# A planner that puts projection products between the steps of four mixers: what is owed is paid in runs instead of piece by piece

## The chip, the cores and the metric

The kernel runs on one core of a Trainium2 chip. The metric is the device time of one execution in microseconds (us), the median of several runs. TensorE multiplies matrices, VectorE (DVE in the profile), ScalarE (ACT) and GpSimd (POOL) do the elementwise work, and DMA queues bring the weights.

## The reference, cut to what matters

One sequence of 512 tokens with 1024 features goes through two layers and then a second block; each has a token mixer and a feed-forward network. All is float32. What the change touches is the mixers, each of which is an input projection followed by work on the projected columns:

```python
z = x @ w_in                        # layer 0: 27 column tiles of 128
y_a = _rwkv7_time_mix(z[..., :RWKV_PROJ_COLS], ...)   # 8 heads of 64, a recurrence over tokens
y_b = moba(...)                     # 4 heads of 128, softmax attention
h = concatenate([y_a, y_b]) @ w_out
...
z = x @ w_in                        # layer 1: 40 column tiles, dilated attention, 8 heads
...
proj = a @ w_in                     # second block: 25 column tiles
y = concatenate([s5(...), hgrn2(...), fox(...), mlstm(...)]) @ w_out
```

## The kernel before

A float32 product is made from three passes: the weights and the activations are each split into a high part in the format fp32r and a remainder, and high times high, high times low and low times high are summed. A **piece** of a projection is the product of one 128x128 block of weights with all 512 tokens, so three matmuls of 512 columns (lines 273 to 275 in `stream`). Eight pieces make one column tile, a task; the weights of the next task are fetched at the first piece and split on ScalarE (line 229) and VectorE (line 231) at the seventh. After a piece `stream` yields 0.64, which is its length in the planner's units. `early` yields pieces of the output projection in the same way (lines 357 to 359).

The mixers are Python generators, called chains. Each step of a chain issues some instructions and yields a pair: what it costs TensorE, and how long until the chain's next step can start, both in the planner's units. The products of a chain are small and plain float32: 16 matmuls of 64x64 (line 560), 64 of 32x32 (lines 611 and 625), four transposes of 128x128 (line 448) and so on.

`race` writes out the order. It keeps a clock `t`, a time `ready` for each chain and a debt `owed`. A chain's step on TensorE adds `keep` times its cost to `owed`; a piece takes 0.64 off it, never below zero. Before each chain step the planner chooses: it issues a piece when no chain is live, when the earliest chain is not ready at `t`, or when `owed` is over 0.6. There are three races: one for layer 0 with five chains (four parts of RWKV, called core, tail with its gate, prep and inner, and the attention heads; keep is 0.65), one for layer 1 with a single chain of heads (keep 0.5), and one for the second block with two chains (keep 0.5). When a stream of pieces is exhausted, `over` supplies the pieces of `early`.

The order that `race` writes is a priority. The framework's own scheduler, while the program is built, places each engine's instructions by that priority as its estimate of readiness allows; on the chip each engine takes its instructions in the order placed, apart from weight loads on TensorE that overlap the products before them.

Of the kernel before, what the change touches and what calls it, by code (L numbers as in the profile page):

```python
# [106 lines left out]
class Kern:  # L107
# [198 lines left out]
    def race(self, chains, over, keep, hop, ls):  # L306


        t, owed, ready, waits, waited, stuck = 0.0, 0.0, [0.0] * len(chains), set(), set(), 0
        while any(chains):  # L310
            ready += [t] * (len(chains) - len(ready))
            live = [i for i, c in enumerate(chains) if c and i not in waits]
            i = min(live, key=lambda j: ready[j]) if live else None
            if self.gemm is not None and (i is None or ready[i] > t or owed > 0.6):
                r = next(self.gemm, None)
                if r is None:
                    self.gemm = over()
                    waits.clear()
                    continue
                if r:  # L320
                    t, owed, stuck = t + r, owed - r, 0
                    owed = max(owed, 0)
                    waits.clear()
                    continue
            if i is None:
                stuck += 1
                assert stuck < 3
                waits.clear()
                continue
            r = next(chains[i][0], 0)  # L330
            if r == 0:
                chains[i].pop(0)
                waits.clear()
            elif r is None:
                waits.add(i)
                waited.add(i)
            else:
                if i in waited:
                    waited.discard(i)
                    ready[i] = max(ready[i], t)  # L340
                at = max(t, ready[i]) if r[0] else ready[i]
                if r[0]:
                    t = at + r[0]
                    owed += keep * r[0]
                ready[i] = at + max(r[0], ls * r[1]) + hop
        while self.gemm is not None:
            if next(self.gemm, None) is None:
                self.gemm = over()
# [2028 lines left out]
```

## Time and profile before

| | |
|---|---|
| median of 3 runs | 2213.09 us (2209.51 to 2214.09) |
| profiled execution | 2210.03 us, its span 2207.9 us |
| busy, of the span | TensorE 97%, VectorE 57%, ScalarE 34%, GpSimd 16% |
| first race | from about 7 us to 397 us; pieces of `stream` until 327 us |
| second race | about 793 to 1119 us |
| third race | about 1498 to 1785 us |

In the rows below a duration of a matmul is partly modelled, and matmuls overlap: what one costs is read from its start to the start of the next one. "x16" in a row of a timeline is 16 instructions in one row, from the first start to the last end.

### The profile page before, as it was taken

What the parts mean: (1) busy time and instruction counts of PE and PEld (TensorE: products, weight loads), DVE (VectorE), ACT (ScalarE), POOL (GpSimd) and SP (SyncE); (2) the same over time, 40 slices, a digit from 0 to 9 for tenths busy, and PEclk for the clock granted to TensorE, in tenths of its full rate; (3) what the DMA queues carried; (4) which work ended last, traced back from release to release, by engine and by line L of the source; (5) the groups of instructions that cost most, each with busy time, mean ns of one, the idle gap of its engine ahead of it and who ended that gap; (6) DMA issues with size and microseconds to landing.
All of it is one profiled execution on the core that took longest, in us unless ns stands there. A gap on an engine that the chain in (4) does not pass through costs nothing.

```text
span 2207.9 us, 37394 instructions
## 1 busy us (share of the span) xinstructions
PE 2146.2 (97%) x15646; PEld 1701.9 (77%) x15646; DVE 1259.3 (57%) x2536; ACT 756.1 (34%) x1214; POOL 363.3 (16%) x391
## 2 busy tenths in 40 slices
PE   8999999999999999999999999998999999999998
PEld 6666667888878787777788888877677778888886
DVE  6575666764444666656474444466856576344445
ACT  4332333423332433333342233235434353222221
POOL 0011011370046433233220000011320021000000
PEclk9999999999999999999999999998999999999999
DMA  4111114333333422222243233213211232232321
GB/s 143 46 44 41 40 44 177 97 121 98 101 101 110 128 81 77 68 77 67 87 139 96 91 98 94 93 44 134 64 49 49 86 112 90 95 97 96 99 81 38
DMA packets 56088, 192.80 MB, mean 87 GB/s; under 512 B 8208, under 2 KB 8720, under 8 KB 55408
## 3 DMA queue, kind: packets, MB, share of 16 engines
q1 hardware_dynamic: 52384, 184.11, 25.9%
q0 software_dynamic: 3536, 6.32, 0.9%
q8 instruction: 122, 2.00, 0.4%
q14 instruction: 46, 0.38, 0.1%
HBM read 181.98 MB, written 8.39 MB: 86 GB/s over the span
## 4 chain that ended last, share of the span: by engine, by line
PE 79%; DVE 11%; issue 4%; ACT 3%; DMA 2%; POOL 1%; SPq 0%; DVEq 0%; ACTq 0%; POOLq 0%
PE gemm L273 6%; PE mlpo L357 6%; PE mlpo L358 6%; PE mlpo L359 6%; PE gemm L274 5%; PE gemm L275 5%; PE mlps L250 5%; PE mlps L251 5%; PE mlps L252 5%; PE ffg L251 2%; PE ffg L252 2%; PE ffg L250 2%; PE ffu L251 2%; PE ffu L252 2%; PE ffu L250 2%
## 5 line engine op out<-in xcount | busy, mean ns | idle before, releaser
L229 ACT CAST wh<-wr 128x1024 fp32r<-128x1024 f32 (+1 forms) x311 | 323.2, 1043 | 758.2 <-PE mlpo L359 241.4
L231 DVE TENSOR_TENSOR wl<-wr,wh 128x1024 fp32r<-128x1024 f32 (+1 forms) x285 | 353.1, 1240 | 354.3 <-ACT wh L229 268.2
L273 PE MATMUL gemm<-acth,wh 128*128 128x512 f32 (+1 forms) x672 | 302.6, 450 | 8.8 <-ACT acth L239 7.5
L275 PE MATMUL gemm<-acth,wl 128*128 128x512 f32 (+1 forms) x672 | 268.9, 400 | 4.4 <-DVE wl L231 4.4
L357 PE MATMUL mlpo<-wh,mlph 128*128 128x512 f32 x688 | 270.1, 393 | 0.2 <-DVE xres L1035 0.2
L274 PE MATMUL gemm<-actl,wh 128*128 128x512 f32 (+1 forms) x672 | 269.7, 401 | 0.0
L358 PE MATMUL mlpo<-wl,mlph 128*128 128x512 f32 x688 | 269.5, 392 | 0.0
L359 PE MATMUL mlpo<-wh,mlpl 128*128 128x512 f32 x688 | 269.4, 392 | 0.0
L250 PE MATMUL mlps<-acth,wh 128*128 128x512 f32 x448 | 176.3, 394 | 0.0
L252 PE MATMUL mlps<-acth,wl 128*128 128x512 f32 x448 | 176.2, 393 | 0.0
L251 PE MATMUL mlps<-actl,wh 128*128 128x512 f32 x448 | 176.1, 393 | 0.0
L273 PEld LDWEIGHTS gemm<-acth,wh 128*128 128x128 f32 (+1 forms) x672 | 126.9, 189 | 56.2 <-issue 19.5
L231 POOL TENSOR_TENSOR wl<-wr,wh 128x1024 fp32r<-128x1024 f32 (+1 forms) x26 | 68.5, 2653 | 553.7 <-ACT wh L229 508.2
L275 PEld LDWEIGHTS gemm<-acth,wl 128*128 128x128 f32 (+1 forms) x672 | 127.1, 189 | 34.9 <-DVE wl L231 5.4
L357 PEld LDWEIGHTS mlpo<-wh,mlph 128*128 128x128 f32 x688 | 129.4, 188 | 29.3 <-ACT mlph L239 0.4
L359 PEld LDWEIGHTS mlpo<-wh,mlpl 128*128 128x128 f32 x688 | 129.1, 188 | 29.1 <-DVE mlpl L240 0.2
L358 PEld LDWEIGHTS mlpo<-wl,mlph 128*128 128x128 f32 x688 | 129.2, 188 | 28.5
L274 PEld LDWEIGHTS gemm<-actl,wh 128*128 128x128 f32 (+1 forms) x672 | 127.7, 190 | 22.4 <-issue 4.6
L1035 DVE SCALAR_TENSOR_TENSOR xres<-xres,mlpo 128x512 f32<-128x512 f32 x120 | 82.1, 685 | 105.2 <-PE mlpo L359 104.1
L252 PEld LDWEIGHTS mlps<-acth,wl 128*128 128x128 f32 x448 | 84.1, 188 | 19.7
L251 PEld LDWEIGHTS mlps<-actl,wh 128*128 128x128 f32 x448 | 84.2, 188 | 19.5
L250 PEld LDWEIGHTS mlps<-acth,wh 128*128 128x128 f32 x448 | 84.1, 188 | 19.5
(613 smaller groups left out, 3874.9 us busy)
## 6 DMA issues: line engine op xcount, KB each, us to landing
wr<-mlp_w SPq DMA_DIRECT2D x128, 512.0 KB, 3.6
wr<-ffn_w SPq DMA_DIRECT2D x66, 512.0 KB, 3.5
wr<-c_w_in SPq DMA_DIRECT2D x40, 512.0 KB, 3.6
wr<-ab_w_in SPq DMA_DIRECT2D x25, 512.0 KB, 3.5
wr<-w_in SPq DMA_DIRECT2D x24, 512.0 KB, 3.7
wr<-ab_w_out SPq DMA_DIRECT2D x8, 512.0 KB, 3.9
wr<-c_w_out SPq DMA_DIRECT2D x8, 512.0 KB, 3.7
wr<-w_out SPq DMA_DIRECT2D x8, 512.0 KB, 4.0
```

Source lines behind the costliest of these rows:

```text
L229: nc.scalar.copy(hi, raw)
L231: eng.tensor_tensor(lo, raw, hi.bitcast(F32), op=ALU.subtract)
L250: nc.tensor.matmul(ps, lhsT=hs, rhs=a, start=start and k == 0, stop=False)
L251: nc.tensor.matmul(ps, lhsT=hs, rhs=b, start=False, stop=False)
L252: nc.tensor.matmul(ps, lhsT=ls, rhs=a, start=False, stop=stop and k == n - 1)
L273: nc.tensor.matmul(ps[0:m], lhsT=h[:, 0:m], rhs=xh[:, k, :], start=k == 0, stop=False)
L274: nc.tensor.matmul(ps[0:m], lhsT=h[:, 0:m], rhs=xl[:, k, :], start=False, stop=False)
L275: nc.tensor.matmul(ps[0:m], lhsT=l[:, 0:m], rhs=xh[:, k, :], start=False, stop=k == n - 1)
L357: nc.tensor.matmul(ps, lhsT=a, rhs=h[:, c0 : c0 + n], start=start and k == 0, stop=False)
L358: nc.tensor.matmul(ps, lhsT=a, rhs=l[:, c0 : c0 + n], start=False, stop=False)
L359: nc.tensor.matmul(ps, lhsT=b, rhs=h[:, c0 : c0 + n], start=False, stop=stop and k == kt - 1)
L1035: self.K.nc.vector.scalar_tensor_tensor(xs, xs, f, ps, op0=ALU.mult, op1=ALU.add, accum_out=self.sums[:, t, c : c + 1])
```

## The change

Until now a piece was issued as soon as `owed` passed 0.6. Now there is a flag `run`: it turns on when `owed` passes 1.3 and stays on until `owed` has come down to zero, and while it is on a piece is issued at every turn. The two other reasons to issue a piece, no live chain and no ready chain, are as before. All three races use this function. Nothing else differs: the same instructions, weights and buffers.

```diff
     def race(self, chains, over, keep, hop, ls):
-        t, owed, ready, waits, waited, stuck = 0.0, 0.0, [0.0] * len(chains), set(), set(), 0
+        t, owed, ready, waits, waited, stuck, run = 0.0, 0.0, [0.0] * len(chains), set(), set(), 0, False
         while any(chains):
             ready += [t] * (len(chains) - len(ready))
             live = [i for i, c in enumerate(chains) if c and i not in waits]
             i = min(live, key=lambda j: ready[j]) if live else None
-            if self.gemm is not None and (i is None or ready[i] > t or owed > 0.6):
+            run = owed > (0.0 if run else 1.3)
+            if self.gemm is not None and (i is None or ready[i] > t or run):
                 r = next(self.gemm, None)
```

## Rows read from the trace of the kernel before

**Rows 1.** The profile's first part: busy time of TensorE and VectorE, share, instructions.
```profile
PE 2146.2 (97%) x15646; PEld 1701.9 (77%) x15646; DVE 1259.3 (57%) x2536; ACT 756.1 (34%) x1214; POOL 363.3 (16%) x391
```

**Rows 2.** Busy time by stretch: first race, its end, second race, third race.
```profile
core 0: us, PE busy (x) PEld busy (x) DVE busy (x) ACT busy (x) POOL busy (x), PEclk, DMA share, GB/s
60.00:328.00 268.00, 265.06 (x4418) 183.27 (x4418) 171.89 (x384) 83.78 (x161) 27.19 (x23) 1.00 0.14 43
328.00:397.00 69.00, 67.25 (x501) 51.28 (x499) 50.05 (x128) 30.34 (x51) 11.78 (x7) 1.00 0.44 153
793.00:1119.00 326.00, 315.02 (x1919) 247.99 (x1918) 204.70 (x466) 121.46 (x212) 99.51 (x66) 0.99 0.24 76
1498.00:1785.00 287.00, 274.76 (x2351) 207.55 (x2352) 178.09 (x400) 124.51 (x226) 40.78 (x66) 0.96 0.23 77
```

**Rows 3.** Groups of TensorE by line in the first race, 60 to 328 us.
```profile
line engine op names shapes xcount | busy us, mean ns | idle before us <-releasers
L273 PE MATMUL gemm<-acth,wh 128*128 128x512 f32 (+1 forms) x167 | 82.9, 496 | 0.0
L274 PE MATMUL gemm<-actl,wh 128*128 128x512 f32 (+1 forms) x167 | 66.7, 399 | 0.0
L275 PE MATMUL gemm<-acth,wl 128*128 128x512 f32 (+1 forms) x167 | 66.3, 397 | 0.0
```

**Rows 4.** The first product of a piece in the second race, 793 to 1119 us.
```profile
L273 PE MATMUL gemm<-acth,wh 128*128 128x512 f32 x288 | 120.2, 417 | 0.0
```

**Rows 5.** The same group in the third race, 1498 to 1785 us.
```profile
L273 PE MATMUL gemm<-acth,wh 128*128 128x512 f32 x168 | 78.2, 466 | 0.7 <-ACT valt L1421 0.7
```

**Rows 6.** TensorE's timeline, first race: start us, us, instruction.
```profile
111.43 0.60 PE L448 MATMUL ptm<-consts,ld 128*128 128x128 f32 x4
111.96 0.76 PE L587 MATMUL pp<-tha,ld 64*32 64x32 f32 x64
112.65 0.50 PE L273 MATMUL gemm<-acth,wh 128*128 128x512 f32 x1
112.98 0.40 PE L274 MATMUL gemm<-actl,wh 128*128 128x512 f32 x1
113.22 0.39 PE L275 MATMUL gemm<-acth,wl 128*128 128x512 f32 x1
113.54 0.68 PE L560 MATMUL pp<-ld,e 64*64 64x64 f32 x16
114.15 0.50 PE L273 MATMUL gemm<-acth,wh 128*128 128x512 f32 x1
...
117.82 0.40 PE L275 MATMUL gemm<-acth,wl 128*128 128x512 f32 x1
118.05 0.40 PE L273 MATMUL gemm<-acth,wh 128*128 128x512 f32 x1
118.29 0.60 PE L769 MATMUL pyt<-consts,yk 128*128 128x128 f32 x4
118.82 0.75 PE L611 MATMUL pinv<-yc,a 32*32 32x32 f32 x64
119.50 0.50 PE L274 MATMUL gemm<-actl,wh 128*128 128x512 f32 x1
```

**Rows 7.** The same timeline, a piece that stands before transposes.
```profile
145.83 0.50 PE L273 MATMUL gemm<-acth,wh 128*128 128x512 f32 x1
...
146.64 0.60 PE L448 MATMUL ptm<-consts,zv 128*128 128x128 f32 x4
```

**Rows 8.** The same timeline, two steps of unlike shape in a row.
```profile
50.50 0.68 PE L560 MATMUL pp<-cum,tha 64*64 64x64 f32 x16
51.11 0.75 PE L625 MATMUL pinv<-pm,xc 32*32 32x32 f32 x64
51.80 0.50 PE L273 MATMUL gemm<-acth,wh 128*128 128x512 f32 x1
```

**Rows 9.** What TensorE waited for, 60 to 328 us: total, times, longest.
```profile
PE pyt L769 <- DVE yk L765: 1.2, 1, 1.2
PE mopt L893 <- DVE mp L885: 1.1, 1, 1.1
PE pb L529 <- DVE rk L524: 0.4, 1, 0.4
PE pinv L625 <- DVE pm L615: 0.2, 1, 0.2
```

**Rows 10.** VectorE's timeline after the step of 118.82 us in rows 6.
```profile
118.54 1.21 DVE L231 TENSOR_TENSOR wl<-wr,wh 128x1024 fp32r<-128x1024 f32 x1
119.68 0.75 DVE L439 SCALAR_TENSOR_TENSOR zr<-gemm,rpar,zr 128x511 f32<-128x511 f32 x1
120.35 0.42 DVE L615 TENSOR_TENSOR pm<-pinv,consts 128x256 f32<-128x256 f32 x1
```

## The prediction

> **What bounds the kernel now.** I read the first part of the profile first: TensorE is busy for 97% of the span, VectorE for 57% [rows 1]. Then the stretches of the three races, since only these contain planned pieces [rows 2]. In the first, between 60 and 328 us, TensorE is busy for 265.06 of 268.00 us and VectorE for 171.89. A busy TensorE is not one that does useful work all the time, so the next view is the groups by line: the three products of a piece have one shape and one size, but the first takes 496 ns on the mean, the others 399 and 397 [rows 3]. The timeline shows why. After a step of a chain the first product's successor starts 0.33 us later (112.65 to 112.98); inside a run the pitch is 0.23 (117.82 to 118.05); and the last product before a step of small tiles again takes 0.33 (113.22 to 113.54) [rows 6]. So a lone piece between such steps holds TensorE for 0.89 us (112.65 to 113.54), a piece inside a run for 3 x 0.23 = 0.69: **going in and out costs 0.20 us**. Before transposes over the full array the exit is free: 0.81 us from 145.83 to 146.64, an overhead of 0.12 [rows 7]. In the second race the first product's mean is 417 ns, in the third 466 [rows 4, 5]: the second is mostly runs already, the third stands between.
>
> In the timeline from 60 to 328 us I count 142 runs of pieces for the 167 pieces of rows 3, and 97 of the runs are exactly one piece (the first such piece of rows 6 is the one at 112.65). By what stands on either side, overheads of 0.20 (about four in five) and 0.1 make a mean of 0.17 us.
>
> **The change, part by part.** It removes and adds no instruction and no transfer; it moves pieces on TensorE. The cost is therefore a number of runs times 0.17, against waits that the new order may open.
>
> *Which pieces it reaches.* A piece is paid for one of three reasons, and only the debt's rule changes. The planner is arithmetic on constants, so its decisions before follow from the code. First race: 16 pieces before any chain is live, 61 because no chain is ready, 130 for the debt, in 123 payments, mostly of one. Second race: none for the debt, which with one chain never passes 0.45; its order stays as it is. Third race: 37 of 192 for the debt.
>
> *How many runs remain.* I follow the new rule by hand from 111.43 us [rows 6]. Twelve steps on TensorE follow, at the planner's 0.45 (transposes), 1.1 (core), 0.65 (inner), 1.1, 0.65, 0.45, 1.1, 0.85, 0.65, 0.85, 1.1, 0.85, in all 9.8, of which 0.65 becomes debt. The old rule paid 10 pieces in 10 places. The new one lets the debt go 0.29, 1.01, 1.43, pays three pieces (1.92, the rest is forgiven), then 0.72, 1.14, 1.43 and pays three, then 0.72, 1.27, 1.69 and three, then 0.55, 1.27, 1.82 and three: 12 pieces in 4 runs. A run replaces 2.5 places, so 123 become about 49, and 74 are saved. Two things give some back. Where a lone chain is live, no debt piece stands behind its step any more, the planner finds it not ready by 0.05 and issues a single piece anyway; following another such stretch I met one in nine units of chain work, and 130 pieces are some 130 x 0.64 / 0.65 = 128 units: 14 more singles, which take the place of five runs, so 9 back. And the framework's scheduler breaks runs up: at 118.05 us it put the transposes and a core step between the first and second product of one piece [rows 6]. Of the 164 runs that I count in the whole first race 34 are broken, no whole number of pieces; I take a sixth of the merged ones, about 12. That leaves 53 x 0.17 = **9.0 us saved**. The bounds: all 74 at 0.20 give 14.8; half of 53 at 0.1 give 2.6.
>
> *The waits it may open.* While a run is saved up, two or three chain steps follow each other with no piece between. The planner prices a core step at 1.1, and the chip takes 0.68 (118.82 to 119.50) [rows 6]: steps without pieces come round faster than the planner thinks. What is then late is VectorE's answer. After the core step of 118.82 its multiplication ran from 120.35 to 120.77, behind 1.2 us of weight splitting and an evacuation [rows 10], so 1.95 us after the step's start. With one inner step of 0.61 us in between (50.50 to 51.11 [rows 8]), the chain's next step would have come 1.29 us after that start: a wait of 0.66, and behind it every other chain and every piece waits, since TensorE takes products in order. Without the backlog the answer (0.75 + 0.42 us) is there in time. So 0 to 0.66 us for each of some 50 intervals, 0 to 33 us. I stay near the lower end: in the present order such neighbours occur too, and TensorE waited for VectorE 2.9 us in 268, in four places [rows 9], because the scheduler puts pieces where it expects a wait. Doubling that adds **3 us**.
>
> *The stream ends sooner.* Twelve pieces for ten bring up to 26 of the 130 forward; the first race's end then has some 26 units of chain work, at most 26 us, more without pieces of the stream. What covers it is the other chains and the 32 pieces of the output projection: from 328 to 397 us TensorE idles 1.75 of 69 us [rows 2], 2.5%. 26 us of that cost 0.65; the singles above forgive nothing, so fewer than 26 come forward, and I take **0.5**.
>
> *The third race.* 37 debt pieces become perhaps 12 runs fewer; its neighbours are often full-array steps, so 0.1 to 0.2 each, 1 to 2 us, and its TensorE already idles 12.24 of 287 us [rows 2]. Net **-1**, between -3 and +3.
>
> Sum: -9.0 + 3 + 0.5 - 1 = **-6.5 us**. The profiled execution took 2210.03 us, 3.06 less than the median of the three runs; against it 2203.5, against the median 2206.6.
>
> **A rule against it.** TensorE pays 0.20 us for a lone piece, and a step of 64x64 tiles takes the same 0.61 us whether a piece or a step of 32x32 tiles follows (113.54 to 114.15; 50.50 to 51.11) [rows 6, 8]. The Trainium skill, "TensorEngine Tiling (Array Packing)", section Key Properties, says that a change of tiling mode drains TensorE. By that rule core and inner steps of unlike tiles, once they are neighbours, still drain between them, and only one of the two drains around a piece goes: 53 x 0.1 = 5.3 instead of 9.0. The trace agrees that a change costs something, and speaks against the halving.
>
> **The rivals.**
> *Half the price*: the step's own duration hides a drain that the new neighbours still pay. The saving is 53 x 0.1 = 5.3, the sum -2.8: 2210.3. One direct neighbourhood, that of rows 8, speaks against it. Chance 0.08.
> *The runs do not form*: the scheduler, by its own estimate of readiness, pulls pieces of a run forward between the chain steps, and TensorE's order stays mostly one by one. For it: the broken piece of rows 6. Against it: most of the present runs follow the planner. A quarter of the saving, 2.3, against the third race's and the end's small terms: within 2 us of before, 2213. Chance 0.14.
> *The chains' answers come late* (slower): each interval between runs waits for VectorE. It decides when the mean wait passes 9.0 / 53 = 0.17 us. At 0.33, half of the 0.66 above, 53 x 0.33 = 17.5 are lost: -9.0 + 17.5 + 0.5 - 1 = +8, 2221. For it: VectorE's 64% of this stretch, in backlogs like that of rows 10. Against it: rows 9. Chance 0.18.
>
> **How the numbers follow.** The forecast of 2206.6 has a chance of 0.60; its own range is 2196 (14.8 saved in the first race and 3 in the third) to 2211 (2.6 saved in the first race, 1 in the third, waits of 2). 0.2% is 4.4 us, about what a measurement of this kernel can tell from no change, so 2208.7 and 2217.5 are the limits. Of the 0.60, 0.52 lies below 2208.7 and 0.08 above. Faster 0.52; same 0.08 + 0.08 + 0.14 = 0.30; slower 0.18. The range runs from 2196 to 2218: the slower rival's far part and what might lie below 2196 are the two in ten left out.
>
> **What would show it.** In the profile after: the mean of line 273 in the first race falls from 496 ns towards 460, since some 53 more of its 167 products stand inside a run at 0.40; runs of exactly one piece fall from 97 to 45 or fewer, and runs of three, of which I count none there now, number 20 or more. The second race keeps its 326 us. The wrong step shows as follows: 496 ns unchanged means that no runs form; a fallen mean with more idle time before the chains' lines (611, 625, 560) means that answers come late; a fallen mean, no idle and no gain means that small-tile steps grew longer beside each other.

## The result and the profile after

The changed kernel takes 2228.97 us (median of 4 runs, 2224.50 to 2231.49) against 2213.59 for the kernel before (4 runs, 2209.51 to 2216.05). The ratio is 1.0066, its 95% interval 1.0047 to 1.0085: slower by some 15 us where 6.5 were to be saved, and outside the range. The profiled execution took 2231.49 us, its span 2229.3. Medians, here and below, count every execution, and ratios leave out three that took far longer (2347.58 us in the third experiment, 5272.1 in the one with keep 0.505, 8514.82 of the kernel before).

Every sign that the prediction named for its runs is there. The first part of the page of the changed kernel comes first, beside [rows 1]: the same instructions, and TensorE busy for 6.7 us more.

```profile
PE 2152.9 (97%) x15646; PEld 1713.1 (77%) x15646; DVE 1258.3 (56%) x2536; ACT 756.7 (34%) x1214; POOL 365.1 (16%) x391
```

The groups by line while the stream lasts, beside [rows 3]. The stream now ends at 308 us, not 327, so the stretch is 60 to 309 us. Line numbers behind the edit are higher by two than before.

```profile
L273 PE MATMUL gemm<-acth,wh 128*128 128x512 f32 (+1 forms) x166 | 74.7, 450 | 0.0
L275 PE MATMUL gemm<-acth,wl 128*128 128x512 f32 (+1 forms) x167 | 66.9, 400 | 0.0
L274 PE MATMUL gemm<-actl,wh 128*128 128x512 f32 (+1 forms) x166 | 66.4, 400 | 0.4 <-issue 0.4
```

The first product's mean fell from 496 to 450 ns. TensorE's timeline of the changed kernel shows why: three pieces in a run between two steps.

```profile
114.78 0.68 PE L562 MATMUL pp<-ld,e 64*64 64x64 f32 x16
115.39 0.50 PE L273 MATMUL gemm<-acth,wh 128*128 128x512 f32 x1
115.73 0.39 PE L274 MATMUL gemm<-actl,wh 128*128 128x512 f32 x1
115.96 0.39 PE L275 MATMUL gemm<-acth,wl 128*128 128x512 f32 x1
116.19 0.40 PE L273 MATMUL gemm<-acth,wh 128*128 128x512 f32 x1
...
117.34 0.39 PE L275 MATMUL gemm<-acth,wl 128*128 128x512 f32 x1
117.66 1.12 PE L470 MATMUL pw<-rwa,wup 64*128 64x512 f32 x2
```

From 115.39 to 117.66 the run holds TensorE for 2.27 us, which is three times 0.69 and once 0.20. From 60 us to the end of the stream the timeline has 85 runs of pieces instead of 142, of exactly one piece 30 instead of 97, and 27 of three instead of none.

The loss lies elsewhere. Busy time by stretch, beside [rows 2]: the stream, what is left of the first race, the second race, the third race.

```profile
core 0: us, PE busy (x) PEld busy (x) DVE busy (x) ACT busy (x) POOL busy (x), PEclk, DMA share, GB/s
60.00:309.00 249.00, 245.06 (x3842) 175.43 (x3843) 162.67 (x364) 80.39 (x153) 26.98 (x22) 0.99 0.15 45
309.00:408.00 99.00, 86.30 (x1094) 64.06 (x1083) 59.38 (x148) 32.81 (x58) 12.66 (x8) 0.91 0.31 107
805.00:1131.00 326.00, 314.61 (x1916) 247.46 (x1915) 203.94 (x470) 122.09 (x212) 101.89 (x66) 0.99 0.24 75
1510.00:1796.00 286.00, 271.71 (x2306) 203.84 (x2306) 168.61 (x377) 121.25 (x221) 40.58 (x66) 0.92 0.23 74
```

The first race ends at 407.6 us, not 396.2, although its stream ended 19 us earlier. (Its end is taken as the first product of the feed-forward network behind it.) What is left after the stream takes 99 us in place of 69, TensorE idles 12.70 us of it in place of 1.75, and its granted clock is 0.91 in place of 1.00 (1 is the higher of TensorE's two levels, 2.4 GHz). The third race, from its first piece to its last output piece, takes 332.0 us in place of 321.7, at a clock of 0.92 in place of 0.96. These two, 11.4 and 10.3 us, are the whole difference of the two profiled executions (21.4 us between spans of 2207.9 and 2229.3). The second race keeps its 326 us.

TensorE's timeline of the changed kernel, in the middle of these 99 us, shows where they go: the end of the attention heads (line 900), a block of output pieces, the last steps of core (lines 717 to 735), its tail (771 to 778).

```profile
342.42 0.49 PE L900 MATMUL mopo<-mpt,mv 128*128 128x128 f32 x2
...
343.50 0.50 PE L359 MATMUL pjps<-wh,acth 128*128 128x512 f32 x1
...
357.93 0.39 PE L361 MATMUL pjps<-wh,actl 128*128 128x512 f32 x1
358.25 0.33 PE L717 MATMUL pst<-state,mt 64*64 64x64 f32 x4
...
361.56 1.28 PE L735 MATMUL py<-state,qtb 64*64 64x64 f32 x31
369.51 1.09 PE L771 MATMUL pyt<-consts,yk 128*128 128x128 f32 x4 [6.67 <-DVE yk L767]
370.40 1.92 PE L776 MATMUL pgt<-zg,gup 128*128 128x512 f32 x2
...
375.74 0.79 PE L359 MATMUL pjps<-wh,acth 128*128 128x512 f32 x1 [1.43 <-ACT acth L239]
```

From 343.50 to 358.25 TensorE does nothing but output pieces, 21 of them. With those that the framework's scheduler placed earlier, 28 of the 32 stand in front of core's last product, where the kernel before had 2.3 (a piece is three products, so there are thirds). Core's last product comes at 362.6 us, not 343.5. Its tail then has nothing beside it. VectorE's timeline at that place is one serial chain, from the first row to the last:

```profile
362.59 0.75 DVE L739 TENSOR_TENSOR yk<-yk,py 128x256 f32<-128x256 f32 x2 [0.49 <-PE py L735]
363.37 0.69 DVE L752 TENSOR_REDUCE gs<-yk 128x8 f32<-128x512 f32 x1
...
368.68 0.69 DVE L767 TENSOR_TENSOR yk<-yk,grs 128x512 f32<-128x512 f32 x1
```

The chain of small operations was there before as well; then the heads and output pieces ran beside it, and TensorE waited 0.52 us. TensorE's timeline of the kernel before:

```profile
342.99 0.69 PE L733 MATMUL py<-state,qtb 64*64 64x64 f32 x18
...
351.82 0.63 PE L769 MATMUL pyt<-consts,yk 128*128 128x128 f32 x4 [0.52 <-DVE yk L765]
```

What TensorE waited for after the stream, in the changed kernel (total, times, longest):

```profile
PE pyt L771 <- DVE yk L767: 6.7, 1, 6.7
PE pjps L359 <- DVE xres L1037: 1.7, 1, 1.7
PE pjps L359 <- ACT acth L239: 1.4, 1, 1.4
```

After the wait of 6.67 us TensorE works at half its clock. In windows over the same place of the changed kernel:

```profile
346.00:370.00 24.00, 16.12 (x138) 13.15 (x137) 13.49 (x33) 6.17 (x7) 0.48 (x1) 0.87 0.40 133
370.00:381.00 11.00, 9.57 (x19) 5.03 (x17) 2.23 (x4) 2.34 (x3) 3.11 (x3) 0.51 0.66 237
```

The granted clock of 0.51 is the lower of the two levels, 1.2 GHz; the products of output pieces there stand 0.43 us apart instead of 0.23. The clock's records have it low from 363.7 us for 17.1 us. A shorter stretch of it, 3.4 us from 302.2 us, follows a wait of 1.93 us at core's step in line 613. The Trainium skill, "TensorE: Matmul & The Clock Gate", section Part 1, says that an idle TensorE drops to half of its clock and gets the rest back only by being busy; these rows agree.

### The profile page after: what moved, and what is told of

Same layout as the page of the kernel before. It is cut to its first block, busy times and chain, and to the rows that moved or that the text cites. A ratio compares the mean times of both kernels' runs of the same rounds, so it can differ in the third digit from the quotient of the medians.

```text
span 2229.3 us, 37411 instructions
## 1 busy us (share of the span) xinstructions
PE 2152.9 (97%) x15646; PEld 1713.1 (77%) x15646; DVE 1258.3 (56%) x2536; ACT 756.7 (34%) x1214; POOL 365.1 (16%) x391
## 4 chain that ended last, share of the span: by engine, by line
PE 65%; DVE 8%; issue 4%; ACT 3%; DMA 1%; POOL 1%; DVEq 0%; SPq 0%; ACTq 0%; POOLq 0%
PE mlpo L359 6%; PE mlpo L360 6%; PE mlpo L361 6%; PE mlps L250 4%; PE mlps L251 4%; PE mlps L252 4%; PE gemm L273 4%; PE gemm L274 3%; PE gemm L275 3%; PE ffg L251 2%; PE ffg L252 2%; PE ffg L250 2%; PE ffu L251 2%; PE ffu L252 2%; PE ffu L250 2%
## 5 line engine op out<-in xcount | busy, mean ns | idle before, releaser
L273 PE MATMUL gemm<-acth,wh 128*128 128x512 f32 (+1 forms) x672 | 297.5, 443 | 7.8 <-ACT acth L239 6.9
```

The lines of the kernel that those rows point to most:

```text
L273: nc.tensor.matmul(ps[0:m], lhsT=h[:, 0:m], rhs=xh[:, k, :], start=k == 0, stop=False)
```

## The experiments

Why do 28 output pieces stand in front of core's last steps? The planner is arithmetic, so its decisions can be followed in the code. Twelve pieces for ten (the debt that a run takes below zero is forgiven) means a faster pace: 18 more pieces were out when the third part of core ended (203 in place of 185, by the traces), and 36.5 units of chain work were left at the stream's end in place of 19.1. In that stretch the heads finished first, at 342.8 us, while core still had its last steps to go. The code lets no output piece out before the chain of the heads is done, so until then the pieces of `early` gave nothing, but each chain step added to the debt. When they came free it was 20.3 units, nearly 32 pieces' worth, and `run` stayed on until all 28 that do not need core's own last result were out, as one block of the plan.

That gave these theories. A: each race loses by itself, for its own reason. B: the first race loses by its pace, which exhausts the stream early. B2, narrower: it loses by the debt that collects while the stream gives nothing. Rival C: runs themselves cost, whatever the pace. Ratios below are to the kernel before on the same chip, with their 95% interval; 0.2% is 4.4 us.

**One race at a time.** In the first experiment the new rule holds in the first race only, in the second in the third race only.

```diff
-            run = owed > (0.0 if run else 1.3)
+            run = owed > ((0.0 if run else 1.3) if keep > 0.6 else 0.6)   # first experiment
+            run = owed > ((0.0 if run else 1.3) if keep < 0.6 else 0.6)   # second
```

> The changed rule in the first race alone; the third race keeps the old rule. In the profiles the first race lost 11 us (end of its pieces 394 us before, 406 after) and the third 10 us. Theory A, each race loses by itself: about 2222 to 2225 us, first race's end near 406 us, third race as long as before (1498 to 1821, 322 us). Rival, the third race's loss is a consequence of how the first one ends (engines, clock): the whole loss stays, about 2229 us.

> The changed rule in the third race alone. Theory A: the first race ends at 394 us as before, the third is 5 to 10 us longer, with more time at the half clock (22 us of it in the third race before, 40 after): 2218 to 2223 us. Rival, the third race's loss was chance of one execution: 2213 us within 3.

Measured, the first: 2223.99 us, 1.0037 (1.0026 to 1.0048), with the first race's end at 405.7 us and the same 28 pieces; the second: 2216.93 us, 1.0015 (1.0005 to 1.0026), with a third race of 331.6 us. Each race loses by itself, and together they make 1.0052, within the interval of the whole change. The first race is the larger part.

**The pace without the runs.** The old rule, one piece at a time, with a keep that brings the pieces forward as far as the new rule does (196 at the end of core's third part, in the planner's own count, either way).

```diff
-RACE_RWKV = (0.65, 0.05, 0.9)
+RACE_RWKV = (0.75, 0.05, 0.9)
```

> The old rule everywhere, single pieces, but keep in the first race 0.75 in place of 0.65, so that the stream of pieces is used up as early as under the change (by the planner's arithmetic 34.1 of 179.0 units of chain work are left when it ends; 36.5 under the change, 19.1 before), and 79, 135 and 196 pieces stand before the ends of the first three cores (78, 135, 196 under the change; 75, 122, 178 before). Theory B, the first race's loss is that the stream ends too soon: it loses the idle time (12 us) and the half clock (3 us) without the 12 us saved on runs, so 2223 to 2230 us. Rival C, the loss comes from the runs themselves (chain steps side by side wait or grow longer): no loss, 2210 to 2215 us.

Measured: 2225.87 us, 1.0040 (1.0023 to 1.0057). The first race ends at 409.9 us, again with 28 output pieces ahead of core's last steps, the wait of 6.7 us, and 17.1 us at half clock. The loss is there with single pieces, so it needs no runs, and B stands. Whether runs cost anything besides (C) is for the next experiment.

**The runs without the pace.** The new rule in the first race with a lower keep, so that 112 pieces are paid for debt; before it was 130, and under the change 160, of which 30 are output pieces. Of the stream 179 pieces are then out at the end of core's third part, in the planner's count (178 before, 196 under the change). The third race goes by the old rule.

```diff
-RACE_RWKV = (0.65, 0.05, 0.9)
+RACE_RWKV = (0.55, 0.05, 0.9)
...
-            run = owed > (0.0 if run else 1.3)
+            run = owed > ((0.0 if run else 1.3) if keep > 0.52 else 0.6)
```

> The changed rule in the first race with keep 0.55 in place of 0.65; the third race keeps the old rule. Pieces then come in 100 runs (168 before, 92 under the change) but as fast as before: 76, 122, 179 pieces before the first three cores' ends, 21.4 units left when the stream ends. Theory B: the saving on runs shows (12 us less on pieces, some 6 us more on chain steps), 2203 to 2208 us. Rival C: no gain or a loss, 2213 to 2222 us.

Measured: 2210.92 us, 0.9977 (0.9968 to 0.9986): faster than before by 5.1 us, somewhat less than expected. The first race ends at 392.1 us, with 3.3 output pieces ahead of core's last product and no time at half clock. The runs do save time when the pace is that of before: C falls.

**No debt while the stream gives nothing.** As the first experiment, but the debt is dropped whenever the stream has nothing to give. Up to the stream's end the order is that of the first experiment.

```diff
                 if r:
                     t, owed, stuck = t + r, owed - r, 0
                     owed = max(owed, 0)
                     waits.clear()
                     continue
+                if keep > 0.6:
+                    owed = 0.0
```

> The changed rule in the first race alone, and in that race the debt is set to zero whenever the stream has no piece to give. Under the change the debt grows while nothing can be paid, and then 28 of the 32 output-projection pieces come in one block in front of the last core's steps; here 8 come in one block and the rest where a chain is not ready. The stream itself ends as early as under the change. Theory B1, what costs is that the input-projection pieces are gone too soon: 2221 to 2226 us as with the changed rule in the first race alone. Theory B2, what costs is that block of 28, which delays the last core and leaves nothing to stand beside its tail: 2212 to 2218 us.

Measured: 2215.76 us, 1.0005 (0.9991 to 1.0020). Ten output pieces stand ahead of core's last product, which comes at 349.4 us; the first race ends at 395.0. TensorE's timeline of this kernel, at the place of the block:

```profile
346.77 0.33 PE L719 MATMUL pst<-state,mt 64*64 64x64 f32 x4
347.03 0.50 PE L361 MATMUL pjps<-wh,acth 128*128 128x512 f32 x1
347.37 0.39 PE L362 MATMUL pjps<-wl,acth 128*128 128x512 f32 x1
347.60 0.40 PE L363 MATMUL pjps<-wh,actl 128*128 128x512 f32 x1
347.93 0.68 PE L737 MATMUL py<-state,qtb 64*64 64x64 f32 x16
```

Single output pieces, where core is not ready, stand in place of the block. That alone takes 10.7 us off the first race of the first experiment (405.7), and the ratio from 1.0037 to 1.0005: B2 holds. It is not the whole: from here to the runs at the old pace (0.9977) 0.28% remain, 6.2 us, and the two intervals do not meet. That part goes with the higher keep; whether by the earlier end of the stream, as B1 has it, is not shown. The profiles show 2.9 us of it in the first race (395.0 against 392.1).

**The third race without forgiving.** The second experiment, with the debt of a run allowed below zero.

```diff
-                    owed = max(owed, 0)
+                    owed = owed if run and keep < 0.6 else max(owed, 0)
```

> The changed rule in the third race alone, with a debt that a run may take below zero, so that a run of three is no more than what is owed. If the third race's 3 us come from pieces issued before their time (theory B carried over): 2212 to 2215 us. If they come from chain steps put side by side (the answers from VectorE late, 3.4 us at the step that forms hgf): 2216 to 2220 us.

Measured: 2218.43 us, 1.0008 (0.9992 to 1.0024), a third race of 331.6 us with 18.7 us idle (16.4 in the second experiment). Inconclusive: the interval holds both theories. By the plan 28 pieces are paid for debt here, against 37 before and 42 in the second experiment, and still the profiled race is as long as with 42.

**Slower paces.** The runs of the fourth experiment with keep 0.505, and single pieces with keep 0.6.

```diff
-RACE_RWKV = (0.55, 0.05, 0.9)
+RACE_RWKV = (0.505, 0.05, 0.9)   # runs; the rule then asks for keep > 0.502
...
-RACE_RWKV = (0.65, 0.05, 0.9)
+RACE_RWKV = (0.6, 0.05, 0.9)     # single pieces, the old rule
```

> As the run with keep 0.55, but keep 0.505: 72, 117, 173 pieces before the first three cores' ends, 14.0 units of chain work left when the stream ends (21.4 with 0.55). Theory B, the later the stream ends the shorter the uncovered end: as fast as or faster than with 0.55, 2204 to 2211 us. Rival, too few pieces between the chains let TensorE wait in the middle of the race: 2212 to 2220 us.

> The old rule, single pieces, with keep 0.6 in place of 0.65: 73, 118, 169 pieces before the first three cores' ends, 11.7 units of chain work left when the stream ends (19.1 before). It separates the pace from the runs on the other side: if a slower pace alone brings what the run with keep 0.55 gained, 2207 to 2211 us, and the runs are worth nothing; if the pace of before was late enough, 2212 to 2216 us, and the gain at keep 0.55 is that of the runs.

Measured: 2220.59 us, 1.0026 (1.0009 to 1.0043), and 2221.66 us, 1.0024 (1.0012 to 1.0035). The first races end at 397.7 and 403.6 us. Both are slower than either expectation had it. Slower is no better: with runs TensorE idles 12.3 us in the first race, against 7.5 in the fourth experiment, and the single pieces meet 10.2 us of half clock at 351.6. The gain of the fourth experiment is therefore the runs', and no pace that the kernel before had missed.

**Single pieces at the fast pace, without the block.** The third experiment with the line of the fifth.

> The old rule with keep 0.75 in the first race, as in e3, and no debt is kept while the stream gives nothing. In e3 the first race ended at 409.9 us, with 28 output-projection pieces in front of the last core's last steps, 16.4 us idle and 17 us at half clock. If the loss of e3 was that block, as in e5, the last core ends some 12 us earlier (352 in place of 364.9), the first race ends between 396 and 402, and the time is 2213 to 2218. If the loss of e3 came from the faster pace before the stream's end, the first race still ends after 406 and the time stays at 2222 or above. Against e5 (395.0, runs of pieces at the same pace): where the runs themselves save time, this one ends its first race 3 to 6 us later than e5.

Measured: 2214.44 us, 1.0000 (0.9991 to 1.0009); the first race ends at 397.1 us, with 11 output pieces ahead of core's last product at 351.9, and no half clock. So the block explains the third experiment too, and with single pieces a faster pace without it costs nothing that can be measured. With runs it costs the 0.28% between the fourth and the fifth experiment, so at this pace the saving of the runs is not seen. Why stays open. The first race ends 2.1 us after that of the fifth experiment, less than the 3 to 6 expected of the runs at this pace, and in the whole time the two don't differ.

**The third race's pace.** The new rule in the third race only, with keep 0.45, so that 36 pieces are paid for debt, as before (37), and not 42.

```diff
-RACE_B = (0.5, 0.1, 1.0)
+RACE_B = (0.45, 0.1, 1.0)
...
-            run = owed > (0.0 if run else 1.3)
+            run = owed > ((0.0 if run else 1.3) if keep < 0.48 else 0.6)
```

> The new rule in the third race alone, with keep 0.45 there in place of 0.5, so that 36 pieces are paid for debt, as before (37), and not 42 as in e2. If the third race loses by its pace, as the first did, its length comes back to 328 us or less with 13 to 15 us idle, and the time is 2211 to 2215. If it loses by late answers of VectorE between the runs, its idle time stays at 16 us or more and its length at 330 or more, and the time is 2216 to 2220.

Measured: 2211.89 us, 0.9990 (0.9979 to 1.0001), a third race of 324.5 us. Its interval and that of the second experiment (1.0005 to 1.0026) don't meet, by 0.0004: the third race's loss goes with its keep. That it is the pace, as in the first race, is not shown: in the plan the second experiment and this one are never more than four pieces apart, and the one without forgiving, with only 28 paid for debt, had a race of 331.6 us too. The windows over the third race, first of the second experiment, then of this one:

```profile
1495.70:1827.30 331.60, 315.19 (x2510) 240.78 (x2509) 203.48 (x461) 145.08 (x263) 51.14 (x71) 0.94 0.25 81
```

```profile
1498.20:1822.80 324.60, 309.52 (x2511) 237.31 (x2509) 203.04 (x462) 144.37 (x263) 51.13 (x71) 0.95 0.25 83
```

The idle time hardly fell (331.60 - 315.19 = 16.4 us to 324.60 - 309.52 = 15.1; 12.2 before), so late answers of VectorE stay. The longest new one is the same under either keep; first the kernel before, then this one:

```profile
PE hgf L1844 <- DVE hfar L1848: 0.6, 1, 0.6
```

```profile
PE hgf L1846 <- DVE hfar L1850: 4.2, 1, 4.2
```

They cost the kernel with keep 0.45 no more than the runs save it. What fell from the second experiment to this one is TensorE's time at half clock, from 36 to 26 us of products, added up from the timeline. Why the clock is low for longer with keep 0.5 stays open.

**Runs in both races at the old pace.** Both keeps lowered in the changed kernel, nothing else.

```diff
-RACE_RWKV = (0.65, 0.05, 0.9)
+RACE_RWKV = (0.55, 0.05, 0.9)
-RACE_B = (0.5, 0.1, 1.0)
+RACE_B = (0.45, 0.1, 1.0)
```

> The changed kernel with keep 0.55 in place of 0.65 in the first race and 0.45 in place of 0.5 in the third, so that both pay about as many pieces for debt as the kernel before. If each race's loss was its pace, the gains of e4 (0.23% below before) and e10 (0.1% below) add up: a ratio of 0.996 to 0.998, some 2205 to 2209 us, with a first race that ends at about 392 us and a third of 324 to 326. If the two are not independent, because the clock of the third race falls elsewhere when it starts earlier, the third race is back at 328 or more and the ratio between 0.998 and 1.0.

Measured: 2207.38 us, 0.9966 (0.9953 to 0.9979): 7.5 us less than before by the ratio, and so faster than both kernels. The two gains add up. The first race ends at 392.2 us and the third takes 325.6. Beside [rows 1], the first part of its page:

```profile
PE 2137.6 (97%) x15646; PEld 1702.5 (77%) x15646; DVE 1255.5 (57%) x2536; ACT 756.8 (34%) x1214; POOL 366.8 (17%) x391
```

TensorE is busy for 8.6 us less than before, with the same 15646 products.

## Why the prediction was wrong

One table carries this part: the first race in the profiled executions, in us. A product's time is taken from its start to the next product's start, less the idle time, and added up by kind; "half" is how much of it ran at half clock. The output pieces are 64 here, since the 32 that follow the planned ones stand before the race's end as well.

| kernel | race ends | pieces | chains' products | output pieces | idle | half | output pieces ahead of core's last product, in number |
|---|---|---|---|---|---|---|---|
| before | 396.2 | 183.1 | 154.0 | 46.0 | 5.6 | 0 | 2.3 |
| after | 407.6 | 171.2 | 163.0 | 48.6 | 17.9 | 13.4 | 28 |
| single pieces, fast pace | 409.9 | 182.1 | 156.3 | 48.6 | 16.4 | 10.3 | 28 |
| runs, old pace | 392.1 | 172.1 | 160.5 | 45.6 | 7.5 | 0 | 3.3 |
| runs, fast pace, no block | 395.0 | 171.2 | 160.3 | 47.4 | 9.3 | 3.6 | 10 |
| single pieces, fast pace, no block | 397.1 | 181.9 | 153.1 | 46.8 | 8.2 | 0 | 11 |

**The step that failed: "The stream ends sooner", 0.5 us.** That pieces come forward, twelve for ten, was seen, and even overestimated: 26 more units of chain work after the stream were forecast, 17.4 came. What failed is the cover. I took TensorE's idle share behind the stream, 2.5% [rows 2], for that of a longer such stretch, with the heads and 32 output pieces as cover. But the heads were used up sooner than core, and 28 of the output pieces were paid in front of it, so the end of the race was a chain with nothing beside it. The block alone, the difference of the first and fifth experiments, measures 0.32% of the time, 7.1 us (10.7 us at the race's end). With the 6.2 us by which the fifth is still behind the fourth, the runs at the faster pace lose some 13 us against those at the old pace; the term had 0.5. Nothing in the rows of before shows it, since there the heads end last (line 898 still runs at 355 us, after core's end at 343.5); it follows from the code, where debt collects while `r` is 0, which I had not followed through to the end of the race.

**The price, 9.0 us.** The order came as forecast: 57 runs fewer while the stream lasts (53 forecast), 30 of one piece (45 or fewer), 27 of three (20 or more), a mean of 450 ns (towards 460). The rival by which the runs do not form falls with that. (The 164 runs that the prediction counts in the whole first race include those of output pieces; this moves nothing.) The pieces' own time fell by 11.0 us in the runs at the old pace. But the chains' products took 6.5 of it back; with the output pieces' 0.4, 4.9 us are saved. All of that growth is in the chains' products on the full array of 128 rows and 128 columns, which rose by 7.1 us, from 42.5 to 49.6; the others together fell by 0.6. It shows in the mean of the heads' products of 128x512, first before, then in the runs at the old pace, both without half clock:

```profile
L898 PE MATMUL mopo<-mpt,mv 128*128 128x512 f32 x8 | 4.1, 592 | 0.0
```

```profile
L900 PE MATMUL mopo<-mpt,mv 128*128 128x512 f32 x8 | 4.5, 640 | 0.0
```

The heads' products and part of the tail's use the full array, as pieces do. While a lone piece stood beside each, the piece paid for the way to the small tiles; without it they pay themselves. In the first race the array changes between full and smaller tiles 296 times before and 242 times in the runs at the old pace. That is 54 fewer, about one for each of the 52 runs saved (output pieces counted in) and not two; at half of 0.20 us each it is 5.4 us. So the price is one of changes, not of runs, and the mean of 0.17 per run was too high. The rival "half the price" (5.3) had the size, but not by the neighbours that it named: it spoke of unlike small tiles beside each other, and what grew are full-array products. The rule of the Trainium skill, "TensorEngine Tiling (Array Packing)", section Key Properties, that a change of mode drains the array, agrees with these rows, at about 0.1 us a change (4.9 us for 54). They do not tell a drain from a load of weights that finds no cover at a change, and between the two small tilings of [rows 8] no such cost shows.

**The waits, +3 us.** From 60 to 309 us TensorE idles 3.94 of 249 us, against 2.94 of 268 before [rows 2, 9]: 1 us more. The longest waits, in the changed kernel:

```profile
PE pinv L613 <- DVE yc L602: 1.9, 1, 1.9
PE pinv L613 <- DVE yc L631: 0.8, 1, 0.8
```

In the runs at the old pace the whole race idles 1.9 us more. The slower rival, late answers in the intervals between runs, would have put its 17.5 us here, and they are not here; the time came out on its side for another reason.

**The second race.** As forecast: 325.6 us, from 325.3. Its pieces, beside [rows 4]:

```profile
L273 PE MATMUL gemm<-acth,wh 128*128 128x512 f32 x288 | 120.8, 419 | 0.0
```

**The third race, -1 us.** By the second experiment it costs 3.3 us (1.1 to 5.8), just beyond the far bound of the forecast. Two things show that it had no term for: a late answer at line 1846, 4.1 us in the changed kernel against 0.6, and the clock. With keep 0.45 in that race the first of them is there too and nothing is lost, so it alone is not the cause. Beside [rows 5], in the changed kernel:

```profile
L273 PE MATMUL gemm<-acth,wh 128*128 128x512 f32 x168 | 80.5, 479 | 0.2 <-ACT valt L1423 0.2
```

The mean rose although the runs formed: the second and third products of a piece, which runs leave almost as they are, rose as well, from 413 to 425 and 426 ns, and the granted clock of the race fell from 0.96 to 0.92. Of the 10.3 us between the two profiled executions a good part is no effect of the change, as the last section shows.

**The sum.** Against -6.5 stand, from the first two experiments, 8.2 in the first race and 3.3 in the third, 11.5 us; the whole change measured 14.6 (10.4 to 18.8). With the pace held, the same rule gives -7.5 (-10.4 to -4.7). The saving was there. That it is about as large as forecast is in part luck, since it comes by other terms: a smaller price, fewer waits, and a third race whose 0.1% cannot be told from none. The pace that came with it, and the block that the pace made, were worth more than twice as much, with the third race's share open in its cause.

## What to carry to other kernels

A rule that pays debts in larger lots and forgives what is overpaid also pays faster: set its rate so that as many pieces as before go out by the same point, and only then judge the lots. Follow a planner's debt through the stretch where nothing can be paid, because all that collects there is paid at once, in front of whatever chain is then the last. And price a change of tiling by counting the changes in the whole order, since a switch that disappears at one product may only move to its neighbour.

## What was not expected of the hardware

A wait in one chain costs TensorE more than its length: after 6.67 us of waiting the products ran at a granted clock of 0.51, 0.43 us apart instead of 0.23, and of the 17.1 us of low clock about ten were spent on work.

The same work takes different times by where the clock is low. With the old rule in the third race, TensorE's order there is the same, and its length in eight profiled executions lies between 321.7 and 328.4 us, with 22 to 33 us of product time at half clock; the kernel before is the shortest. A difference of 3 us between two single profiles of that stretch says nothing; only the intervals of the timed runs do.
